# Causal masks added to the score banks by an identity matmul in a two-layer hybrid attention trunk

## Chip, cores and metric

The kernel runs on one core of one Trainium2 chip. The time is device microseconds of one execution of the whole program, the median of three runs. What the core has: TensorE (PE for its matmuls, PEld for the loads of their stationary operand), VectorE (DVE), ScalarE (ACT), GpSimd (POOL), SyncE (SP, which issues most DMAs here), SBUF, and eight PSUM banks of 128 partitions x 512 float32.

## The reference

A trunk of two layers on x of 512 rows x 1024 columns. In each layer: an RMSNorm and one input projection; from it four heads of differential attention with rotary (two softmax maps per head, subtracted) and eight heads of stick-breaking attention; the two results are projected, gated, merged and projected again; then a SwiGLU FFN. The two kinds of causal mask are what this change is about:

```python
# differential: a key may be the query itself
mask = kpos[None, :] <= qpos[:, None]
sc = einsum('bhqd,bhkd->bhqk', qb, k) * scale
w = softmax(where(mask, sc, -inf))
# stick-breaking: keys before the query only
mask = kpos[None, :] < qpos[:, None]
z = einsum('bhqd,bhkd->bhqk', qb, k) * scale
log_beta = log_sigmoid(z)
log_rem = where(mask, log_sigmoid(-z), 0.0)
after = cumsum(log_rem, reverse=True) - log_rem
a = where(mask, exp(log_beta + after), 0.0)
```

## The kernel before

All activations are kept transposed (features on partitions, the 512 tokens along the free axis). A projection is made in groups: 128 output features, eight steps of 128 input features, and for each step three float32r matmuls of 512 columns, because weight and activation are each split into a high and a low float32r part (L204: high x high, L205: weight low x high, L206: weight high x activation low). So a group is 24 matmuls. Its weight block comes by one DMA (L110), is rounded by ACT (L111) and its low part is made by DVE or, for some blocks, POOL (L113).

Attention goes by eight units a layer: four of the stick-breaking kind (s0 to s3, `class SB`), then four of the differential kind (d0 to d3, `class Diff`). A unit has two halves, c = 0 and 1. For each half, `scores` (L397) writes the causal part of the 512 x 512 score matrix, four blocks of rows of 128 queries with 128, 384, 512 and 256 keys, into three PSUM banks (L405 and L406: key high and key low; a query's two parts lie on the two halves of the partitions). Then `maps`:

- Stick-breaking (L428): ACT makes e = sigmoid(-z/8) and z = sigmoid(z/8) from the banks (L435, L437). POOL multiplies z on the four diagonal blocks with a 0/1 mask (L441). DVE runs a scan along e, from the last key to the first, with a second operand that holds it at 1 on masked places (L443). POOL multiplies z with the scanned e (L445).
- Differential (L472): DVE adds a mask of 0 and -1e30 to the diagonal blocks in PSUM (L481), takes row maxima (L482, L483), ACT exponentiates with row sums (L487), DVE and POOL scale (L489 to L496).

Two halves later (`LAG`), `mix` transposes the map on PE into three banks (L419), splits it (L422 on ACT, L423 on DVE), and multiplies it with the values (L456, L457; L512 to L514); the result is read by L461 (ACT) and L462 (DVE), or normalised through a matmul of ones (L525, L526) and L152 to L156. Projection groups of the next unit and of the gates stand between these steps as work for PE. Pools: five banks (`at`) for scores, transposes, values and norms together, three (`mm`) for projections, four buffers of the maps (`wk`).

The order of each engine's instructions is not the written one: a scheduler in the layer that records the kernel runs its own estimate of the timeline and lays each engine's queue down in that order. On the chip each engine goes through its queue in order. So taking instructions out, or putting some in, moves others.

Of the kernel before, what the change touches and what calls it, by code (L numbers as in the profile page):

```python
# [8 lines left out]
F32 = mybir.dt.float32  # L9
F32R = mybir.dt.float32r  # L10
BF16 = mybir.dt.bfloat16
AF = mybir.ActivationFunctionType
ALU = mybir.AluOpType
AX = mybir.AxisListType

P = 128
# [4 lines left out]
HID = 2816  # L21
NH = HID // P
EPS = 1e-6
NEG = -1.0e30


SEG = {0: (0, 0, 0, 128), 2: (0, 128, 128, 384), 3: (1, 0, 512, 512), 1: (2, 0, 1024, 256)}
# [20 lines left out]
def trunk(ctx: ExitStack, tc, xT, par, tab, scn, msk, w_in, w_o, w_out, w_fi, w_fo, out):  # L48
    nc = tc.nc
    cst = ctx.enter_context(tc.tile_pool(name="cst", bufs=1))  # L50
# [5 lines left out]
    def bank(tag, name):  # L56
        return psm.tile([P, 512], F32, name=name, tag=tag, bufs=BANK_BUFS[tag])
# [72 lines left out]
    ident = cst.tile([P, P], F32, name="ident")  # L130
# [95 lines left out]
            pass  # L226
    for k in range(KT):
        nrm.square(k)
    mk = cst.tile([P, 2, P], F32, name="mk")
    nc.sync.dma_start(out=mk, in_=msk)  # L230
    lam = cst.tile([P, DEPTH], F32, name="lam")
    gsub = cst.tile([P, DEPTH], F32, name="gsub")
    lctx = ExitStack()
    lcst = lctx.enter_context(tc.tile_pool(name="lcst", bufs=1))
    lpt = lcst.tile([P, DEPTH, 2, 2, 64], F32, name="lpt")
    nc.sync.dma_start(out=lpt.rearrange("p l a b d -> p (l a b d)"), in_=par[:, C_LP:])
    lpp = lcst.tile([P, DEPTH, 2, 64], F32, name="lpp")
    lps = lcst.tile([P, DEPTH, 2], F32, name="lps")
    for l in range(DEPTH):
# [6 lines left out]
                                       in1=lps[:, l, 0:1], op0=ALU.add, op1=ALU.subtract)  # L246
# [11 lines left out]
    def fbank(name):  # L258
        t = free_tags[fcount[0] % len(free_tags)]
        fcount[0] += 1  # L260
        return bank(t, name)

    for l in range(DEPTH):
        h = nrm.h
        with ExitStack() as ac:
# [10 lines left out]
            def T(tag, name, shape=(P, S), dt=F32):  # L276
                return ap_.tile(list(shape), dt, name=f"{name}_{l}", tag=tag, bufs=BUFS.get(tag, 1))
# [41 lines left out]
            class Unit:  # L319
# [77 lines left out]
                def scores(self, c):  # L397
                    ka, kl = self.k[c], self.k[2][c]
                    qs = self.q[c]
                    bs = [bank("at", f"s{self.n}{c}{i}_{l}") for i in range(3)]  # L400
                    for qb in (0, 2, 3, 1):
                        bi, c0, _, n = SEG[qb]
                        qc = slice(qb * P, qb * P + P)
                        dst = bs[bi][:, c0:c0 + n]
                        nc.tensor.matmul(dst, qs[:, qc], ka[:, 0:n], start=True, stop=False)  # L405
                        nc.tensor.matmul(dst, qs[:, qc], kl[:, 0:n], start=False, stop=True)  # L406
                    return bs

                def transposed(self, w, name):
# [17 lines left out]
            class SB(Unit):  # L427
                def maps(self, c):  # L428
                    name = f"{self.n}{c}"
                    bs = self.scores(c)  # L430

                    e = T("wk", "e" + name, (P, 1280))
                    z = T("wk", "z" + name, (P, 1280))
                    for i, (o, n) in enumerate(BANKS):
                        nc.scalar.activation(out=e[:, o:o + n], in_=bs[i][:, :n], func=AF.Sigmoid, scale=-0.125)  # L435
                    for i, (o, n) in enumerate(BANKS):
                        state["sig"] = nc.scalar.activation(out=z[:, o:o + n], in_=bs[i][:, :n], func=AF.Sigmoid,  # L437
                                                            scale=0.125)
                    for o in (0, 384, 896, 1152):
                        d = z[:, o:o + P]  # L440
                        nc.gpsimd.tensor_tensor(out=d, in0=d, in1=mk[:, 1], op=ALU.mult)  # L441

                    nc.vector.tensor_tensor_scan(out=e[:, ::-1], data0=e[:, ::-1], data1=msc[:, ::-1], initial=1.0,  # L443
                                                 op0=ALU.mult, op1=ALU.max)
                    nc.gpsimd.tensor_tensor(out=z[:, 0:1279], in0=z[:, 0:1279], in1=e[:, 1:1280], op=ALU.mult)  # L445
                    return z
# [24 lines left out]
            class Diff(Unit):  # L471
                def maps(self, c):  # L472
                    name = f"{self.n}{c}"
                    bs = self.scores(c)
                    p = T("wk", "p" + name, (P, 1280))
                    mx = T("mx", "mx" + name, (P, 4))
                    sm = T("sm", "sm" + name, (P, 4))
                    for qb in (0, 2, 3, 1):
                        bi, c0, s0, n = SEG[qb]
                        d = bs[bi][:, c0 + n - P:c0 + n]  # L480
                        nc.vector.tensor_tensor(out=d, in0=d, in1=mk[:, 0], op=ALU.add)  # L481
                        nc.vector.tensor_reduce(out=mx[:, qb:qb + 1], in_=bs[bi][:, c0:c0 + n], axis=AX.X, op=ALU.max)  # L482
                    nc.vector.tensor_scalar(out=mx, in0=mx, scalar1=-0.125, scalar2=None, op0=ALU.mult)  # L483
                    for qb in (0, 2, 3, 1):
                        bi, c0, s0, n = SEG[qb]
                        with tc.issue_after(state["tab"].ins):
                            nc.scalar.activation(out=p[:, s0:s0 + n], in_=bs[bi][:, c0:c0 + n], func=AF.Exp,  # L487
                                                 scale=0.125, bias=mx[:, qb:qb + 1], accum_out=sm[:, qb:qb + 1])
                    nc.vector.reciprocal(out=sm, in_=sm)  # L489
                    if c == 1:  # L490
                        nc.vector.tensor_scalar(out=sm, in0=sm, scalar1=lam[:, l:l + 1], scalar2=None, op0=ALU.mult)
                    else:
                        for qb in (0, 2, 3, 1):
                            bi, c0, s0, n = SEG[qb]
                            nc.gpsimd.tensor_scalar(out=p[:, s0:s0 + n], in0=p[:, s0:s0 + n],
                                                    scalar1=sm[:, qb:qb + 1], scalar2=None, op0=ALU.mult)  # L496
                    return p, sm
# [85 lines left out]
            for m in range(8):  # L583
                hi, lo = w_get(l, "o", m)
                bs, bd = fbank(f"ws{m}_{l}"), fbank(f"wd{m}_{l}")
# [88 lines left out]
def _constants(np):  # L674
    pos = np.arange(S, dtype=np.float32)
    inv = np.float32(10000.0) ** (-np.arange(0, 64, 2, dtype=np.float32) / np.float32(64))
    ang = pos[None, :] * inv.astype(np.float32)[:, None]
    cos, sin = np.cos(ang), np.sin(ang)
    tab = np.stack([np.concatenate([cos] * 4), np.concatenate([sin, -sin] * 2)], axis=1).astype(np.float32)
    q, k = np.arange(P)[:, None], np.arange(P)[None, :]  # L680
    msk = np.stack([np.where(k <= q, 0.0, NEG), np.where(k < q, 1.0, 0.0)], axis=1).astype(np.float32)
    scn = np.zeros((P, 1280), np.float32)
    for o in (0, 384, 896, 1152):
        scn[:, o:o + P] = 1.0 - msk[:, 1]
    return np.ascontiguousarray(tab), scn, np.ascontiguousarray(msk)


# [32 lines left out]
```

## Time and profile before

| | |
|---|---|
| median of 3 runs | 1538.57 us (1538.2 to 1538.72) |
| the profiled execution | 1538.29 us, of which its span, first to last instruction, 1536.5 us |
| PE busy in the span | 1482.3 us (96%), 6756 matmuls |
| DVE, ACT, POOL busy | 873.2 (57%), 611.3 (40%), 412.6 us (27%) |
| attention of layer 0, of layer 1 | about 45 to 300 us, about 790 to 1050 us |
| TensorE's clock over the span | 0.983 of full |

A time stands for a start in us from the first instruction, a duration beside it in us. A matmul's duration overlaps that of the next one, so what a matmul costs in a stream is the distance from its start to the next start. The clock has two levels, 2.4 GHz (1.0) and 1.2 GHz (0.5); a granted clock in between is a mean over a stretch.

### The profile page before, as it was taken

The numbers are of one execution on the slowest core, as the hardware profiler recorded it, in microseconds if no ns is written. First come the engines' busy times: TensorE is split into PE (matmuls) and PEld (weight loads), VectorE is DVE, ScalarE is ACT, GpSimd is POOL, SyncE is SP. The second block draws the span as 40 slices with busy tenths as digits, with TensorE's granted clock in tenths as the row PEclk, the third lists the DMA queues.
The fourth block names the chain that finished last, engine by engine and source line by source line (L and its number), as shares of the span: only waits on it lengthen the run. The fifth ranks groups of instructions, "written<-read, shape, count | busy, mean of one in ns | idle before, by whom it ended". The sixth has DMA issues, their size and how long they took to land.

```text
span 1536.5 us, 17374 instructions
## 1 busy us (share of the span) xinstructions
PE 1482.3 (96%) x6756; PEld 1228.0 (80%) x6756; DVE 873.2 (57%) x1070; ACT 611.3 (40%) x968; POOL 412.6 (27%) x288
## 2 busy tenths in 40 slices
PE   8899989999999999999997989999999999999997
PEld 6777778888888888888886867788888888888886
DVE  5978777565454544423367778765755454544223
ACT  5546445453332322322235645536434222333231
POOL 4679444000111111101128765520011111111011
PEclk8999999999999999999999999999999999999999
DMA  6212222223332323333331212322332323232331
GB/s 206 69 58 69 87 77 82 82 96 96 96 96 96 96 96 96 93 100 100 93 109 42 76 55 73 113 69 71 114 102 85 104 91 106 92 101 90 99 94 61
DMA packets 43619, 139.59 MB, mean 91 GB/s; under 512 B 5648, under 2 KB 8080, under 8 KB 43536
## 3 DMA queue, kind: packets, MB, share of 16 engines
q1 hardware_dynamic: 42240, 137.38, 28.7%
q8 instruction: 53, 0.87, 0.2%
q10 hardware_dynamic: 1296, 1.09, 0.2%
q14 instruction: 30, 0.25, 0.1%
HBM read 132.16 MB, written 2.10 MB: 87 GB/s over the span
## 4 chain that ended last, share of the span: by engine, by line
PE 79%; DVE 8%; POOL 5%; issue 3%; ACT 2%; DMA 1%; SPq 1%; DVEq 0%; POOLq 0%; ACTq 0%
PE fg L204 5%; PE fu L204 5%; PE fg L205 5%; PE fu L205 5%; PE fu L206 5%; PE fg L206 5%; PE fo L204 5%; PE fo L206 5%; PE fo L205 5%; PE pg L206 3%; PE pg L205 3%; PE pg L204 3%; PE wo L205 2%; PE wo L206 2%; PE wo L204 2%
## 5 line engine op out<-in xcount | busy, mean ns | idle before, releaser
L111 ACT CAST wh<-wr 128x1024 fp32r<-128x1024 f32 (+3 forms) x251 | 258.2, 1029 | 608.5 <-PE fu L206 153.6
L113 DVE TENSOR_TENSOR wl<-wr,wh 128x1024 fp32r<-128x1024 f32 (+2 forms) x229 | 327.7, 1431 | 208.1 <-ACT wh L111 207.6
L625 POOL TENSOR_TENSOR u<-u,g 128x512 f32<-128x512 f32 x44 | 57.9, 1316 | 440.4 <-DVE u L624 383.3
L205 PE MATMUL fo<-ah,wl 128*128 128x512 f32 (+1 forms) x374 | 141.0, 377 | 0.0
L204 PE MATMUL fo<-ah,wh 128*128 128x512 f32 (+1 forms) x374 | 141.0, 377 | 0.0
L206 PE MATMUL fo<-al,wh 128*128 128x512 f32 (+1 forms) x374 | 140.8, 376 | 0.0
L204 PE MATMUL fg<-hhf,wh 128*128 128x512 f32 x352 | 137.7, 391 | 0.0
L206 PE MATMUL fu<-hlf,wh 128*128 128x512 f32 x352 | 136.9, 389 | 0.0
L205 PE MATMUL fg<-hhf,wl 128*128 128x512 f32 x352 | 136.9, 389 | 0.0
L206 PE MATMUL fg<-hlf,wh 128*128 128x512 f32 x352 | 136.9, 389 | 0.0
L204 PE MATMUL fu<-hhf,wh 128*128 128x512 f32 x352 | 136.9, 389 | 0.0
L205 PE MATMUL fu<-hhf,wl 128*128 128x512 f32 x352 | 136.9, 389 | 0.0
L624 DVE TENSOR_TENSOR u<-fu,yf 128x512 f32<-128x512 f32 x44 | 30.4, 691 | 129.5 <-PE fu L206 129.5
L204 PE MATMUL pg<-hha,wh 128*128 128x512 f32 x256 | 101.4, 396 | 0.0
L206 PE MATMUL pg<-hla,wh 128*128 128x512 f32 x256 | 101.3, 396 | 0.0
L205 PE MATMUL pg<-hha,wl 128*128 128x512 f32 x256 | 101.3, 396 | 0.0
L205 PEld LDWEIGHTS fo<-ah,wl 128*128 128x128 f32 x374 | 70.4, 188 | 13.1
L206 PEld LDWEIGHTS fo<-al,wh 128*128 128x128 f32 x374 | 70.4, 188 | 13.0
L204 PEld LDWEIGHTS fo<-ah,wh 128*128 128x128 f32 x374 | 70.4, 188 | 12.7
L204 PE MATMUL pd<-hha,wh 128*128 128x512 f32 x192 | 77.1, 402 | 2.6 <-ACT knd3s L336 2.6
L113 POOL TENSOR_TENSOR wl<-wr,wh 128x1024 fp32r<-128x1024 f32 (+3 forms) x22 | 49.0, 2229 | 108.4 <-ACT wh L111 94.4
L187 POOL TENSOR_TENSOR accf<-accf,sqf 128x512 f32<-128x512 f32 x10 | 18.5, 1846 | 220.0 <-ACT sqf L185 220.0
(266 smaller groups left out, 3197.4 us busy)
## 6 DMA issues: line engine op xcount, KB each, us to landing
wr<-in_w_fi_dram SPq DMA_DIRECT2D x88, 512.0 KB, 3.5
wr<-in_w_in_dram SPq DMA_DIRECT2D x78, 512.0 KB, 3.5
wr<-in_w_fo_dram SPq DMA_DIRECT2D x32, 512.0 KB, 3.5
wr<-in_w_o_dram SPq DMA_DIRECT2D x16, 512.0 KB, 3.5
wr<-in_w_out_dram SPq DMA_DIRECT2D x16, 512.0 KB, 3.5
wr<-in_w_fo_dram SPq DMA_DIRECT2D x16, 384.0 KB, 3.1
x<-in_xT_dram SPq DMA_DIRECT2D x8, 256.0 KB, 5.3
cs<-in_tab_dram SPq DMA_DIRECT2D x2, 512.0 KB, 5.0
```

Of the source, the lines that this page charges most:

```text
L111: nc.scalar.copy(out=hi[:, c], in_=raw[:, c])
L113: eng.tensor_tensor(out=lo[:, c], in0=raw[:, c], in1=f32(hi[:, c]), op=ALU.subtract)
L187: eng.tensor_tensor(out=self.acc, in0=self.acc, in1=sq, op=ALU.add)
L204: nc.tensor.matmul(dst, hi[:, c], rh, start=first and k == 0, stop=False)
L205: nc.tensor.matmul(dst, lo[:, c], rh, start=False, stop=False)
L206: nc.tensor.matmul(dst, hi[:, c], rl, start=False, stop=last and k == n - 1)
L624: nc.vector.tensor_tensor(out=u, in0=bu, in1=r, op=ALU.mult)
L625: nc.gpsimd.tensor_tensor(out=u, in0=u, in1=g, op=ALU.mult)
```

## The change

The masks become one more matmul in each block of scores. `mk` is cast to float32r and holds 0 and -2^100 for both kinds (the stick-breaking one was 1 and 0); an identity in float32r, `identr`, is the stationary operand; behind the two score matmuls of each of the four row blocks a third one of 128 columns adds the mask to the diagonal block in PSUM. The POOL products (L441) and the DVE additions (L481) go. sigmoid and exp then give 0 or 1 on masked places by themselves. Two casts on ACT are added at the start.

```diff
--- before.py
+++ after.py
@@ -21,7 +21,7 @@
 HID = 2816
 NH = HID // P
 EPS = 1e-6
-NEG = -1.0e30
+NEG = -2.0 ** 100
 
 
 SEG = {0: (0, 0, 0, 128), 2: (0, 128, 128, 384), 3: (1, 0, 512, 512), 1: (2, 0, 1024, 256)}
@@ -226,12 +226,17 @@
             pass
     for k in range(KT):
         nrm.square(k)
-    mk = cst.tile([P, 2, P], F32, name="mk")
-    nc.sync.dma_start(out=mk, in_=msk)
     lam = cst.tile([P, DEPTH], F32, name="lam")
     gsub = cst.tile([P, DEPTH], F32, name="gsub")
     lctx = ExitStack()
     lcst = lctx.enter_context(tc.tile_pool(name="lcst", bufs=1))
+
+    mkf = lcst.tile([P, 2, P], F32, name="mkf")
+    nc.sync.dma_start(out=mkf, in_=msk)
+    mk = cst.tile([P, 2, P], F32R, name="mk")
+    nc.scalar.copy(out=mk, in_=mkf)
+    identr = cst.tile([P, P], F32R, name="identr")
+    nc.scalar.copy(out=identr, in_=ident)
     lpt = lcst.tile([P, DEPTH, 2, 2, 64], F32, name="lpt")
     nc.sync.dma_start(out=lpt.rearrange("p l a b d -> p (l a b d)"), in_=par[:, C_LP:])
     lpp = lcst.tile([P, DEPTH, 2, 64], F32, name="lpp")
@@ -403,7 +408,8 @@
                         qc = slice(qb * P, qb * P + P)
                         dst = bs[bi][:, c0:c0 + n]
                         nc.tensor.matmul(dst, qs[:, qc], ka[:, 0:n], start=True, stop=False)
-                        nc.tensor.matmul(dst, qs[:, qc], kl[:, 0:n], start=False, stop=True)
+                        nc.tensor.matmul(dst, qs[:, qc], kl[:, 0:n], start=False, stop=False)
+                        nc.tensor.matmul(dst[:, n - P:], identr, mk[:, int(self.kind == "s")], start=False, stop=True)
                     return bs
 
                 def transposed(self, w, name):
@@ -436,9 +442,6 @@
                     for i, (o, n) in enumerate(BANKS):
                         state["sig"] = nc.scalar.activation(out=z[:, o:o + n], in_=bs[i][:, :n], func=AF.Sigmoid,
                                                             scale=0.125)
-                    for o in (0, 384, 896, 1152):
-                        d = z[:, o:o + P]
-                        nc.gpsimd.tensor_tensor(out=d, in0=d, in1=mk[:, 1], op=ALU.mult)
 
                     nc.vector.tensor_tensor_scan(out=e[:, ::-1], data0=e[:, ::-1], data1=msc[:, ::-1], initial=1.0,
                                                  op0=ALU.mult, op1=ALU.max)
@@ -477,8 +480,6 @@
                     sm = T("sm", "sm" + name, (P, 4))
                     for qb in (0, 2, 3, 1):
                         bi, c0, s0, n = SEG[qb]
-                        d = bs[bi][:, c0 + n - P:c0 + n]
-                        nc.vector.tensor_tensor(out=d, in0=d, in1=mk[:, 0], op=ALU.add)
                         nc.vector.tensor_reduce(out=mx[:, qb:qb + 1], in_=bs[bi][:, c0:c0 + n], axis=AX.X, op=ALU.max)
                     nc.vector.tensor_scalar(out=mx, in0=mx, scalar1=-0.125, scalar2=None, op0=ALU.mult)
                     for qb in (0, 2, 3, 1):
@@ -678,10 +679,10 @@
     cos, sin = np.cos(ang), np.sin(ang)
     tab = np.stack([np.concatenate([cos] * 4), np.concatenate([sin, -sin] * 2)], axis=1).astype(np.float32)
     q, k = np.arange(P)[:, None], np.arange(P)[None, :]
-    msk = np.stack([np.where(k <= q, 0.0, NEG), np.where(k < q, 1.0, 0.0)], axis=1).astype(np.float32)
+    msk = np.stack([np.where(k <= q, 0.0, NEG), np.where(k < q, 0.0, NEG)], axis=1).astype(np.float32)
     scn = np.zeros((P, 1280), np.float32)
     for o in (0, 384, 896, 1152):
-        scn[:, o:o + P] = 1.0 - msk[:, 1]
+        scn[:, o:o + P] = msk[:, 1] != 0.0
     return np.ascontiguousarray(tab), scn, np.ascontiguousarray(msk)
```

Counts: 32 score halves (2 layers, 8 units, 2 halves) of four row blocks make 128 new matmuls with 128 new loads; 64 POOL and 64 DVE instructions go. (Lines behind L236 have other numbers in the changed kernel: L441 and L481 are gone, L445 is L448, L405 and L406 are L410 and L411, the mask is L412, L336 is L341, L487 is L488, L419 is L425, L526 is L527.)

What stands where, in three places. In a name such as zs01 the digits are the unit and the half, in ss102 the unit, the half and the bank; the number behind the last underscore is a buffer's.

POOL's queue in the first stick-breaking halves of layer 0, before:

```order
L376 TENSOR_TENSOR qbs0_0_343<-qns0_0_340,qbs0_0_343 64x512
L441 TENSOR_TENSOR zs00_0_372<-zs00_0_372,mk_192 128x128 x3
L375 TENSOR_TENSOR qas1_0_459<-qns1_0_457,qas1_0_459 64x512
L441 TENSOR_TENSOR zs00_0_372<-zs00_0_372,mk_192 128x128
L376 TENSOR_TENSOR qbs1_0_460<-qns1_0_457,qbs1_0_460 64x512
L441 TENSOR_TENSOR zs01_0_477<-zs01_0_477,mk_192 128x128 x2
L445 TENSOR_TENSOR zs00_0_372<-zs00_0_372,es00_0_371 128x1279
L441 TENSOR_TENSOR zs01_0_477<-zs01_0_477,mk_192 128x128 x2
L445 TENSOR_TENSOR zs01_0_477<-zs01_0_477,es01_0_476 128x1279
L375 TENSOR_TENSOR qas2_0_665<-qns2_0_663,qas2_0_665 64x512
L376 TENSOR_TENSOR qbs2_0_666<-qns2_0_663,qbs2_0_666 64x512
L441 TENSOR_TENSOR zs10_0_545<-zs10_0_545,mk_192 128x128 x4
```

and now:

```order
L381 TENSOR_TENSOR qbs0_0_347<-qns0_0_344,qbs0_0_347 64x512
L380 TENSOR_TENSOR qas1_0_463<-qns1_0_461,qas1_0_463 64x512
L381 TENSOR_TENSOR qbs1_0_464<-qns1_0_461,qbs1_0_464 64x512
L448 TENSOR_TENSOR zs00_0_380<-zs00_0_380,es00_0_379 128x1279
L448 TENSOR_TENSOR zs01_0_485<-zs01_0_485,es01_0_484 128x1279
L448 TENSOR_TENSOR zs10_0_553<-zs10_0_553,es10_0_552 128x1279
L380 TENSOR_TENSOR qas2_0_669<-qns2_0_667,qas2_0_669 64x512
L381 TENSOR_TENSOR qbs2_0_670<-qns2_0_667,qbs2_0_670 64x512
L113 TENSOR_TENSOR wl12_877<-wr12_875,wh12_876 128x1024
L448 TENSOR_TENSOR zs11_0_691<-zs11_0_691,es11_0_690 128x1279
```

The mask products are gone; the product with the scanned e stands directly behind the query splits (L380, L381).

ACT's queue at the differential unit d2 of layer 0, before (omd0 is the bank of d0's norm, pd30 a projection bank of d3, sd200 to sd202 the scores of d2's first half):

```order
L152 ACTIVATE yod0_0_1812<-omd0_0_1805,eps_81 128x512
L153 ACTIVATE yod0_0_1812<-yod0_0_1812 128x512
L336 COPY knd3s_0_1918<-pd30_0_1885 128x512
L487 ACTIVATE pd20_0_1864,smd20_0_1866<-sd200_0_1853,mxd20_0_1865 128x128
L487 ACTIVATE pd20_0_1864,smd20_0_1866<-sd200_0_1853,mxd20_0_1865 128x384
L487 ACTIVATE pd20_0_1864,smd20_0_1866<-sd201_0_1854,mxd20_0_1865 128x512
L487 ACTIVATE pd20_0_1864,smd20_0_1866<-sd202_0_1855,mxd20_0_1865 128x256
L336 COPY qnd3s_0_1968<-pd31_0_1935 128x512
L111 CAST wh29_2178<-wr29_2177 128x1024
```

and now:

```order
L152 ACTIVATE yod0_0_1816<-omd0_0_1809,eps_81 128x512
L153 ACTIVATE yod0_0_1816<-yod0_0_1816 128x512
L488 ACTIVATE pd20_0_1872,smd20_0_1874<-sd200_0_1857,mxd20_0_1873 128x128
L488 ACTIVATE pd20_0_1872,smd20_0_1874<-sd200_0_1857,mxd20_0_1873 128x384
L488 ACTIVATE pd20_0_1872,smd20_0_1874<-sd201_0_1858,mxd20_0_1873 128x512
L488 ACTIVATE pd20_0_1872,smd20_0_1874<-sd202_0_1859,mxd20_0_1873 128x256
L341 COPY knd3s_0_1922<-pd30_0_1889 128x512
L341 COPY qnd3s_0_1972<-pd31_0_1939 128x512
```

The exponentials of d2's first half moved ahead of the copy that frees the projection bank pd30.

PE's queue at the same place, from the second half's first scores to the projection group pd32, before:

```order
L405 MATMUL sd210_0_1983<-kbd2_0_1637,qbd2_0_1687 128x384
L406 MATMUL sd210_0_1983<-klz01_0_323,qbd2_0_1687 128x384
L526 MATMUL omd0_0_1805<-old0_0_1807,ones_v_79 128x512
L204 MATMUL pd32_0_2012<-hha00_110,wh25_1887 128x512
L205 MATMUL pd32_0_2012<-hha00_110,wl25_1888 128x512
L206 MATMUL pd32_0_2012<-hla00_111,wh25_1887 128x512
```

and now:

```order
L410 MATMUL sd210_0_1987<-kbd2_0_1641,qbd2_0_1691 128x384
L411 MATMUL sd210_0_1987<-klz01_0_327,qbd2_0_1691 128x384
L412 MATMUL sd210_0_1987<-mk_199,identr_201 128x128
L410 MATMUL sd211_0_1988<-kbd2_0_1641,qbd2_0_1691 128x512
L411 MATMUL sd211_0_1988<-klz01_0_327,qbd2_0_1691 128x512
L412 MATMUL sd211_0_1988<-mk_199,identr_201 128x128
L410 MATMUL sd212_0_1989<-kbd2_0_1641,qbd2_0_1691 128x256
L411 MATMUL sd212_0_1989<-klz01_0_327,qbd2_0_1691 128x256
L412 MATMUL sd212_0_1989<-mk_199,identr_201 128x128
L204 MATMUL pd32_0_2016<-hha00_110,wh25_1891 128x512
L205 MATMUL pd32_0_2016<-hha00_110,wl25_1892 128x512
```

The rest of the second half's scores (sd211, sd212), which stood 22 projection matmuls later, now stands ahead of pd32. Elsewhere: between the last score matmul of s1's first half and the first transposes of the kernel (of zs00), 12 projection matmuls stood before and 9 stand now.

## Rows read from the trace of the kernel before

**Rows 1.** Busy time by stretch, us: PE, PEld, DVE, ACT, POOL; clock; DMA; GB/s
```profile
45.00:150.00 105.00, 94.60 (x456) 78.41 (x455) 85.21 (x79) 60.82 (x114) 84.90 (x56) 0.93 0.19 61
150.00:300.00 150.00, 143.20 (x682) 119.11 (x681) 108.53 (x190) 67.40 (x144) 59.74 (x41) 0.97 0.27 81
790.00:910.00 120.00, 105.14 (x518) 86.66 (x518) 92.54 (x90) 64.90 (x120) 86.47 (x58) 0.97 0.22 70
910.00:1050.00 140.00, 132.49 (x636) 110.72 (x635) 102.50 (x184) 65.26 (x138) 58.01 (x39) 0.98 0.27 83
...
300.00:784.00 484.00, 484.00 (x2135) 400.39 (x2134) 225.54 (x242) 162.05 (x205) 52.44 (x37) 1.00 0.31 96
```
**Rows 2.** Waits of PE in the four attention stretches: us in total, times, longest
```profile
PE ts L419 <- POOL zs L445: 4.6, 1, 4.6
...
PE avs L457 <- DVE tls L423: 7.4, 3, 3.8
PE ts L419 <- POOL zs L445: 4.4, 1, 4.4
...
PE ts L419 <- DVE os L462: 2.7, 1, 2.7
PE sd L405 <- DVE os L462: 2.1, 1, 2.1
PE pd L204 <- ACT knd3s L336: 2.0, 1, 2.0
...
PE pd L204 <- ACT knd3s L336: 0.6, 1, 0.6
```
**Rows 3.** Timeline of PE behind the first stall: start, us, instruction
```profile
72.33 1.12 PE L419 MATMUL ts<-ident,zs 128*128 128x128 f32 x4 [4.64 <-POOL zs L445]
73.09 0.78 PE L206 MATMUL ps<-hla,wh 128*128 128x512 f32 x1
...
77.02 0.39 PE L206 MATMUL ps<-hla,wh 128*128 128x512 f32 x1
```
**Rows 4.** Timelines of DVE and POOL around two PE stalls
```profile
59.24 3.81 DVE L443 TENSOR_TENSOR_SCAN es<-es,msc 128x1280 f32<-128x1280 f32 x1 [1.70 <-ACT es L435]
...
60.45 2.86 POOL L441 TENSOR_TENSOR zs<-zs,mk 128x128 f32<-128x128 f32 x1
...
66.71 5.56 POOL L445 TENSOR_TENSOR zs<-zs,es 128x1279 f32<-128x1279 f32 x1
...
830.43 2.78 POOL L445 TENSOR_TENSOR zs<-zs,es 128x1279 f32<-128x1279 f32 x1
...
830.93 2.83 DVE L368 TENSOR_TENSOR klz<-kns,kbs 64x512 fp32r<-64x512 f32 x1
```
**Rows 5.** The mask products on POOL: times, duration in ns min/median/max
```profile
L441 POOL TENSOR_TENSOR zs<-zs,mk x64: 449/466/3303, 57.6 to 907.0; 128x128 f32<-128x128 f32 x64
```
**Rows 6.** Timeline of PE in the first scores of layer 0
```profile
52.74 0.22 PE L405 MATMUL ss<-kas,qas 128*128 128x128 f32 x1
52.80 0.28 PE L406 MATMUL ss<-klz,qas 128*128 128x128 f32 x1
52.91 0.39 PE L405 MATMUL ss<-kas,qas 128*128 128x384 f32 x1
```
**Rows 7.** Timelines of DVE and ACT in the first differential map
```profile
163.53 0.29 DVE L481 TENSOR_TENSOR sd<-sd,mk 128x128 f32<-128x128 f32 x1
163.72 0.68 DVE L482 TENSOR_REDUCE mxd<-sd 128x1 f32<-128x512 f32 x1
...
167.08 0.37 ACT L487 ACTIVATE pd<-sd,mxd 128x128 f32<-128x128 f32 x1 [7.90 <-DVE mxd L483]
...
169.10 0.62 ACT L373 CAST qad<-qnd 64x512 fp32r<-64x512 f32 x1
```
**Rows 8.** Timeline of ACT near the start: [idle before <- released by]
```profile
2.76 0.30 ACT L111 CAST wh<-wr 128x128 fp32r<-128x128 f32 x1 [0.32 <-DMA wr<-in_w_in_dram]
...
20.44 0.40 ACT L242 ACTIVATE lps<-lps 128x2 f32<-128x2 f32 x2 [3.99 <-DVE lps L241]
```

## The prediction

> **What bounds the kernel now.** I read the busy times by stretch first [rows 1]. Outside attention PE is busy without a gap at full clock (484.00 of 484 us between 300 and 784), so nothing there can be won, and the change touches nothing there. In the four attention stretches PE is idle for 105 - 94.60 = 10.4, 150 - 143.20 = 6.8, 120 - 105.14 = 14.9 and 140 - 132.49 = 7.5 us: 25.3 us in the stick-breaking parts (45 to 150 and 790 to 910), 14.3 us in the differential parts.
>
> The second thing to see in [rows 1] is the clock: 0.93, 0.97, 0.97 and 0.98. Behind the longest stalls PE goes on at the lower of its two levels. In [rows 3] nine matmuls of 512 columns take from 73.09 to 77.02, 3.93 us; at full clock 2135 matmuls take 484 us [rows 1], 0.227 us each, so nine take 2.04, and the stall of 4.64 us cost a further 1.9 us. Over the stretches the clock gives away 105 x 0.07 + 120 x 0.03 = 11.0 us in the stick-breaking parts and 150 x 0.03 + 140 x 0.02 = 7.3 in the differential ones. About 1 us of it falls on time in which PE was idle anyway, which leaves 10.4 and 6.9. So PE's stalls are worth 25.3 + 10.4 = 35.7 us in the stick-breaking parts and 21.2 us in the differential ones. That is all that a change to the masks' engines can win. What it costs is PE time, and PE is the bound.
>
> Third, who ends those waits [rows 2]: twice the product L445 on POOL (4.6 and 4.4), and for the rest mostly DVE: splits of transposes (7.4 in three waits between 790 and 910), the sums L462 (2.7 and 2.1 between 150 and 300). In the stick-breaking parts POOL is busy 84.9 of 105 and 86.5 of 120 us, DVE 85.2 and 92.5 [rows 1]: two loaded engines that stretch each other. The mask product takes 0.449 us at best and 3.303 at worst [rows 5]; a DVE instruction that starts inside a POOL product of 2.78 us is itself 2.83 us long [rows 4].
>
> **What the change adds on PE.** 128 matmuls of 128 columns in float32r, each with its own load. The nearest rows are the two 128-column score matmuls of the same type [rows 6]: the second starts 0.06 us behind the first, and the matmul behind it 0.11 us later. So a mask costs 0.06 us where the loads around it are hidden by long matmuls, 0.11 us where they aren't, as behind the 128-column block or where the next block's load is pushed back. Ends: 128 x 0.06 = 7.7 and 128 x 0.11 = 14.1 us. I take the middle, 0.085, 10.9 us, since 32 of them stand behind short blocks and the others push the next load. Below 7.7 it goes only if masks fall into stalls that last until another engine is ready; that is counted with the stalls.
>
> The Trainium skill, page "TensorE: Matmul & The Clock Gate", section "Back-to-back issue gap", gives about 81 ns for a matmul of 128 columns in a stream with its loads; by that the term would be an estimated 10.4 us, inside the ends above.
>
> **What it takes off POOL and DVE.** POOL loses 64 products, 64 x 0.466 = 30 us by the median, and more with what contention adds. In the first half of layer 0 the chain is plain: a mask product of 2.86 us at 60.45, the scan done at 59.24 + 3.81 = 63.05, L445 only at 66.71 and 5.56 us long [rows 4], the transposes at 72.33 [rows 3]. POOL's queue now has the query splits and then L445 directly. Without four masks on the way, L445 can start when the scan is done, 3.7 us earlier, and in an emptier stretch of DVE. So I take the two waits named POOL as gone, each with the 1.9 us of clock: 4.6 + 4.4 + 3.8 = 12.8 us.
>
> The rest of the stick-breaking stalls, 35.7 - 12.8 = 22.9 us, ends on DVE and ACT work that was late for a mixture of reasons: products in front of the query splits and of the rotary steps on POOL, DVE instructions stretched by POOL. The masks are one part of it. L445, which stays, is another: at 830.93 it was L445 and not a mask that stretched the DVE instruction ahead of the late split [rows 4]. I take half, 11.4 us. Ends: nothing and all of it. Together 24.2 us.
>
> **The differential parts.** The 64 DVE additions take 0.289 us each, but the next instruction starts 0.19 us later [rows 7], so a half wins 4 x 0.19 = 0.8 us on DVE's queue. Two PE waits hang on a DVE sum L462 in these stretches [rows 2]; in the first map it stands behind such additions: 1.6 us less.
>
> Against it stands d2. PE waits there for the copy that frees a projection bank (2.0 us in layer 0, 0.6 in layer 1) [rows 2]. Now four exponentials stand ahead of that copy on ACT; the first map's take from 167.08 to 169.10, 2.0 us [rows 7]. Of that PE spends about 0.9 us on the scores moved into the place. So the wait grows by 1.1 us a layer, 2.2 us, and layer 1's wait, then 1.7 us, may bring a lower clock for another 1.9. I take +3.1; the part as a whole +1.5 us, with ends -4 (the queue is ahead in more places) and +5.
>
> **The start.** Two casts are added on ACT. The identity's 128 x 128 cast costs 0.3 us by the row of the same shape and stands in an idle 0.32 us before the first weight cast; the mask's falls before a wait of 3.99 us [rows 8]. Both are hidden, at most 0.1 us late. The mask's DMA is the same one. FFN and projections behind attention keep their work: 0.
>
> **The sum.** The profiled execution is 1538.29 us (span 1536.5 and 1.8 around it), 0.3 below the median. +10.9 - 24.2 + 1.5 = -11.8, so 1526.5 us, beside the median 1526.8. I say 1527.
>
> **Rivals.** *The cover is taken back (slower).* The scheduler lays the queues by its own estimate, in which POOL's products may never have been late. It put the first transposes behind 9 projection matmuls instead of 12, some 0.7 us less cover, and crowded d2's scores. If new waits open in other places for all that closes, the stalls stay at 57 us, PE pays 10.9, the differential part 1.5: 1538.3 + 12.4 = 1551 us. It decides from the point where the stick-breaking stalls shrink by less than 12.4 us. For it speaks that stalls are set by an order made with wrong durations, against it that POOL had 81% load and now has half of that.
>
> *Only POOL's own two waits go.* The waits that end on DVE stay, since L445 still stretches DVE: 10.9 - 12.8 + 1.5 = -0.4, 1538 us. The Trainium skill, page "SBUF — State Buffer", section "Who interferes with whom", says that a VectorE instruction with two SBUF inputs and a GpSimd instruction that reads SBUF exclude each other for the whole instruction, whoever starts first; the 2.83 us at 830.93 agree, and by it the long POOL product goes on blocking as before.
>
> *Nearly all stick-breaking stalls go*, and the matmuls cost little: 9 - 34 - 2 = -27, 1511 us. For it speaks that POOL's queue feeds query splits, rotary steps and L445 alike.
>
> *It doesn't do what it says* is out: the order shows the 64 + 64 instructions gone and 128 matmuls there.
>
> **Chances.** About 0.2% (3 us) is what a measurement of this kernel can tell from no change. Forecast, 1518 to 1535: 0.42. Nearly all stalls gone, below 1518: 0.16. Only the two waits, 1535.5 to 1541.5: 0.14. Cover taken back, above 1541.5: 0.28. So faster 0.58, same 0.14, slower 0.28. Range: the low end is 10.9 - 35.7 less a few in the differential part, 1508; the high end the cover rival, 1551. About one in ten lies on either side.
>
> **What would show it.** In the changed kernel's waits of PE, the two named POOL zs should be gone, PE idle in the stick-breaking stretches should be about 11 instead of 25.3 us, with a clock of 0.97 or more; POOL's busy time should fall by 50 to 65 us. Mask matmuls should start 0.06 to 0.11 us before the next matmul. At d2 PE should wait 2 to 3 us for the copy or the exponentials. It is wrong if PE's idle time in attention stays near 40 us, or if a mask costs over 0.11 us.

## The result and the profile after

The changed kernel takes 1526.28 us (median; 1523.85 to 1527.29), the kernel before 1538.38 in the same comparison: 0.9921 of the time, 95% interval 0.9904 to 0.9938. Forecast were 1527. The profiled execution has a span of 1525.0 us (before 1536.5), TensorE's mean clock is 0.988 (0.983). The total came out as forecast; the terms did not, and most of what follows is about that.

The page's first part for the changed kernel, busy us by engine:

```profile
PE 1488.5 (98%) x6884; PEld 1238.6 (81%) x6884; DVE 853.7 (56%) x1006; ACT 614.4 (40%) x970; POOL 347.4 (23%) x224
```

POOL lost 65.2 us, DVE 19.5. The stretches of [rows 1] again, in the same columns:

```profile
45.00:150.00 105.00, 98.32 (x505) 83.55 (x504) 85.35 (x85) 61.56 (x115) 53.94 (x26) 0.95 0.20 61
150.00:300.00 150.00, 147.94 (x731) 124.62 (x731) 99.83 (x161) 75.55 (x153) 57.37 (x38) 0.99 0.27 85
790.00:910.00 120.00, 110.72 (x560) 92.65 (x558) 95.72 (x96) 67.30 (x128) 62.04 (x33) 0.96 0.21 65
910.00:1050.00 140.00, 137.93 (x678) 116.37 (x677) 92.47 (x144) 69.73 (x139) 50.87 (x32) 0.99 0.27 82
```

PE's idle time is now 6.7 and 9.3 us in the stick-breaking stretches (25.3 together before, 16.0 now) and 2.1 and 2.1 in the differential ones (14.3 before, 4.1 now). The larger part of the idle time that went was in the parts where the prediction expected none to go. Who ends PE's waits (us in total, times, longest; compare [rows 2]):

```profile
PE avs L460 <- DVE tls L429: 7.9, 4, 3.0
PE ts L425 <- DVE vs L398: 4.0, 1, 4.0
PE sd L410 <- ACT pd L488: 3.6, 2, 1.8
...
PE ss L410 <- DVE vs L398: 1.6, 1, 1.6
...
PE ts L425 <- POOL zs L448: 0.5, 1, 0.5
PE pd L204 <- ACT knd3s L341: 0.5, 2, 0.2
```

The two waits named POOL zs (4.6 and 4.4) have shrunk to one of 0.5. The large ones left end on DVE. Two DVE timelines of the changed kernel (start, us; the second is in layer 1), and the POOL products beside them:

```profile
64.56 2.56 DVE L371 CAST kbs<-kns 64x512 fp32r<-64x512 f32 x1
...
69.72 2.83 DVE L446 TENSOR_TENSOR_SCAN es<-es,msc 128x1280 f32<-128x1280 f32 x1
72.46 0.40 DVE L398 TENSOR_TENSOR vs<-vts,vs 128x256 fp32r<-128x256 f32 x1
...
73.65 4.17 DVE L446 TENSOR_TENSOR_SCAN es<-es,msc 128x1280 f32<-128x1280 f32 x1
...
813.67 2.26 DVE L370 CAST kas<-kns 64x512 fp32r<-64x512 f32 x1
815.94 0.42 DVE L371 CAST kbs<-kns 64x512 fp32r<-64x512 f32 x1
...
819.30 2.83 DVE L446 TENSOR_TENSOR_SCAN es<-es,msc 128x1280 f32<-128x1280 f32 x1
822.04 0.67 DVE L429 TENSOR_TENSOR tls<-ts,ths 128x512 fp32r<-128x512 f32 x1
```

```profile
64.32 2.52 POOL L448 TENSOR_TENSOR zs<-zs,es 128x1279 f32<-128x1279 f32 x1
...
813.20 2.45 POOL L448 TENSOR_TENSOR zs<-zs,es 128x1279 f32<-128x1279 f32 x1 [3.96 <-DVE es L446]
```

The small instruction that PE waits for, a value split (L398) or a transpose split (L429), stands behind a scan of 2.8 us. In layer 0 a second value split hangs on the first through a cast on ACT (72.89, which had waited 4.94 us for it), and the transposes follow at 73.87. POOL is idle meanwhile (5.85 us up to 72.69, 6.64 up to 822.29), so the order in DVE's queue has a part in these waits. But POOL has one too, some microseconds earlier: the key splits at 64.56 and 813.67 start inside a product L448 and take 2.56 and 2.26 us, where a key split of the same size at 815.94, with POOL idle, takes 0.42. DVE has no pause from there to the split that PE waits for, so up to 2.1 and 1.8 us of the two waits can be POOL's. No run takes the two shares apart.

### The profile page after: what moved, and what is told of

The parts are those of the page before. It is cut to its first block, busy times and chain, and to the rows that moved or that the text cites. A ratio compares the mean times of both kernels' runs of the same rounds, so it can differ in the third digit from the quotient of the medians.

```text
span 1525.0 us, 17531 instructions
## 1 busy us (share of the span) xinstructions
PE 1488.5 (98%) x6884; PEld 1238.6 (81%) x6884; DVE 853.7 (56%) x1006; ACT 614.4 (40%) x970; POOL 347.4 (23%) x224
## 4 chain that ended last, share of the span: by engine, by line
PE 90%; DVE 5%; issue 1%; ACT 1%; DMA 1%; POOL 0%; SPq 0%; DVEq 0%; POOLq 0%; ACTq 0%
PE fu L206 5%; PE fg L205 5%; PE fg L206 5%; PE fu L205 5%; PE fg L204 5%; PE fu L204 5%; PE fo L204 5%; PE fo L205 5%; PE fo L206 5%; PE pg L204 4%; PE pg L205 4%; PE pg L206 4%; PE pd L204 3%; PE pd L205 3%; PE pd L206 3%; PE wo L204 2%
## 5 line engine op out<-in xcount | busy, mean ns | idle before, releaser
L205 PE MATMUL pd<-hha,wl 128*128 128x512 f32 x192 | 77.7, 405 | 0.0
```

The lines of the kernel that those rows point to most:

```text
L205: nc.tensor.matmul(dst, lo[:, c], rh, start=False, stop=False)
```

## The experiments

Four theories were set against each other: the products taken off POOL (A); the additions taken off DVE (B); the order in which the scheduler lays the queues down, which any edit moves (C); that the work alone decides, whatever the order (W). The before that each time is set against was run beside it (1537.1 to 1538.0 us). Executions of one kernel lie 1 to 7 us apart, so a few microseconds between two of the kernels below are little.

**One half of the change.** Masks by matmul in the stick-breaking units alone, the DVE additions kept:

```diff
-nc.tensor.matmul(dst, qs[:, qc], kl[:, 0:n], start=False, stop=False)
-nc.tensor.matmul(dst[:, n - P:], identr, mk[:, int(self.kind == "s")], start=False, stop=True)
+nc.tensor.matmul(dst, qs[:, qc], kl[:, 0:n], start=False, stop=self.kind != "s")
+if self.kind == "s":
+    nc.tensor.matmul(dst[:, n - P:], identr, mk[:, int(self.kind == "s")], start=False, stop=True)
...
```

> Only the stick-breaking masks go by the matmul (64 of 128); the differential ones stay additions on DVE. Theory A (the prediction's: the gain is POOL's relief in the stick-breaking parts): 5.4 us of PE for -24, about 1520 us. Theory B (from the two traces: idle time of PE fell by 9 us in the stick-breaking parts, by 10 us and most of the lower clock in the differential ones, so the DVE additions were what counted): -9 + 5.4, about 1534 us. Theory C (the new order of the queues counts, not the work taken off): any value, and the changes of this run and of e2_diff_only don't add up to that of the whole change (-12 us).

Measured: 1516.8 us, 0.9859 (0.9842 to 0.9875), 9.5 us better than the whole change. And the reverse, with `"d"` for `"s"` and the POOL products kept:

> Only the differential masks go by the matmul; the stick-breaking ones stay products on POOL. Theory A: PE pays 5.4 us and 1.5 come on top, about 1545 us. Theory B: -15 + 5.4, about 1529 us. Theory C: no sum with e1_stick_only.

Measured: 1536.4 us, 0.9993 (0.9983 to 1.0002), no change. PE's waits for the POOL product are both there (first line layer 0, second layer 1):

```profile
PE ts L428 <- POOL zs L454: 5.0, 1, 5.0
...
PE ts L428 <- POOL zs L454: 4.4, 1, 4.4
```

The halves give -20.8 and -1.2, together -22, the whole change -12: they do not add up. Of the forecasts, A's for the first half (1520) was met, A's for the second (1545) and both of B's (1534 and 1529) were not. PE's waits of the first half alone in layer 0 (45 to 300 us):

```profile
PE ts L426 <- DVE vs L398: 4.0, 1, 4.0
PE pd L204 <- ACT knd3s L341: 2.0, 1, 2.0
PE avs L461 <- DVE tls L430: 1.9, 2, 1.7
PE ts L426 <- POOL zs L449: 0.3, 1, 0.3
```

Nothing there ends on the sums any more (L462 in [rows 2]), although all DVE additions are still in place: B falls for the differential stalls.

**The change with the old work put back.** First all 64 POOL products (they multiply by 1 or 0 what is masked already), then all 64 DVE additions:

```diff
...
+for o in (0, 384, 896, 1152):
+    d = z[:, o:o + P]
+    nc.gpsimd.tensor_tensor(out=d, in0=d, in1=m01, op=ALU.mult)
```

> The changed kernel with the 64 POOL products on the diagonal blocks put back as well (they multiply what is already 0). So PE pays for all masks and POOL has no relief. Theory A: the gain of 24 us is gone, about 1551 us. Theory B: only the differential gain stays, about 1534 us.

Measured: 1530.39 us, 0.9953 (0.9937 to 0.9968).

```diff
+d = bs[bi][:, c0 + n - P:c0 + n]
+nc.vector.tensor_tensor(out=d, in0=d, in1=f32(mk[:, 0]), op=ALU.add)
```

> The changed kernel with the 64 DVE additions put back as well (the mask is added twice). Theory A: +2 us, about 1528 us. Theory B: the differential gain of 15 us is gone, about 1541 us.

Measured: 1522.28 us, 0.9904 (0.9889 to 0.9919). A had forecast 1551 and 1528, B 1534 and 1541. The first is the differential half (1536.4) with 64 more matmuls in it, and 6 us faster than that; the second is the changed kernel with 64 more additions, and 4 us faster than that, 3 us if each is set against its own before, with intervals that overlap. The work added can't explain a gain; the queues of both stand in another order. But little of it is idle time of PE (the table below has 2.7 us less in the first, 1.0 us more in the second); the rest is a better clock, in the second 0.98, 0.97, 1.00 and 1.00 in the four windows of the table (two stick-breaking, two differential), against 0.95, 0.95, 0.99 and 0.99 in the changed kernel. So the second shows neither work nor order. In it, PE's wait at d2 is 0.5 us in each layer, for the copy, against 1.8 for the exponentials in the changed kernel. Against the stick-breaking half it has 64 masks more, and is 5.5 us slower; that is no clean price of a mask either, since the half ran at a lower clock (0.95, 0.95, 0.99 and 1.00).

**The order alone.** Two edits that change no instruction, only the sequence in which they are written, and with it the scheduler's order (616 and 602 rows of PE's queue differ in the kernel before):

```diff
-                    for qb in (0, 2, 3, 1):
+                    for qb in (0, 2, 1, 3):
```

> The kernel before with the same instructions; only the written order of the last two row blocks in the scores is swapped (0, 2, 1, 3), which makes the scheduler lay the queues down otherwise (616 rows of PE's queue differ). Theory W (the work taken off or added counts): within 3 us of 1537.5. Theory C (the order of the queues counts as much): more than 4 us away, to either side.

> The changed kernel with the swap of o1_before_scores_order. Theory W: within 3 us of 1526 and 11 us below o1_before_scores_order. Theory C: the distance to o1_before_scores_order is not 11 us but anything between 0 and 25.

```diff
-                    for i, kbs in enumerate(((0,), (1, 3), (2,))):
+                    for i, kbs in ((0, (0,)), (2, (2,)), (1, (1, 3))):
```

> The kernel before with the same instructions; only the three banks of the transposes are written in the order 0, 2, 1 (602 rows of PE's queue differ). Theory W: within 3 us of 1537.5. Theory C: more than 4 us away.

> The changed kernel with the swap of o2_before_transposes_order. Theory W: within 3 us of 1526 and 11 us below o2_before_transposes_order. Theory C: the distance to o2_before_transposes_order is not 11 us but anything between 0 and 25.

> The kernel with masks by matmul in the stick-breaking part alone (1516.8 with the order as written), with the row blocks of a head's scores written in the order 0, 2, 1, 3 instead of 0, 2, 3, 1. The work is the same to the last instruction; the order of the queues is another. If the gain of 21 us over the kernel before comes from the work taken off GpSimd, it stays: 1513 to 1521. If it is to a good part a lucky order, as the runs of the two kernels with this swap suggest (the kernel before 1542, the changed one 1534), then the time moves toward theirs: 1523 to 1533.

> The same kernel with the three banks of the transposes written in the order 0, 2, 1. This swap took the kernel before from 1538 to 1523 and left the changed kernel at 1526. If what the swap gives and what the smaller change gives were separate, they would add up: 1517 - 15 = 1502. If both remove the same stalls, or the order alone decides, the time lies at 1513 to 1526. Slower than 1530 would say that this part of the change has no gain of its own over the kernel before with the same swap (1523).

Measured, with all other kernels. PE's idle us are the length less PE's busy time of the windows that begin with the first score matmul of the first stick-breaking or differential unit of a layer, and end with that of the next kind or the output projection, both layers together, in the profiled execution of each kernel:

| kernel | us | ratio to before (95%) | idle, stick-breaking | idle, differential |
|---|---|---|---|---|
| before | 1538.4 | | 25.2 | 14.4 |
| before, scores order | 1542.4 | 1.0023 (1.0013 to 1.0033) | 23.5 | 19.4 |
| before, transposes order | 1523.2 | 0.9903 (0.9889 to 0.9918) | 21.1 | 10.6 |
| changed | 1526.3 | 0.9921 (0.9904 to 0.9938) | 16.0 | 4.1 |
| changed, scores order | 1533.6 | 0.9979 (0.9968 to 0.9989) | 17.0 | 11.8 |
| changed, transposes order | 1526.0 | 0.9918 (0.9903 to 0.9933) | 15.9 | 6.7 |
| stick-breaking half | 1516.8 | 0.9859 (0.9842 to 0.9875) | 15.6 | 3.4 |
| same, scores order | 1535.4 | 0.9990 (0.9980 to 0.9999) | 16.9 | 19.5 |
| same, transposes order | 1516.5 | 0.9868 (0.9854 to 0.9883) | 15.2 | 7.3 |
| differential half | 1536.4 | 0.9993 (0.9983 to 1.0002) | 21.3 | 9.4 |
| products kept | 1530.4 | 0.9953 (0.9937 to 0.9968) | 19.0 | 9.0 |
| additions kept | 1522.3 | 0.9904 (0.9889 to 0.9919) | 16.6 | 4.5 |

Three things are to be read from it. The order alone moves the kernel before by 19 us (1523.2 to 1542.4), more than the change does; W falls and C stands. Over the three orders the change is worth -12.1, -8.8 and +2.8 us, its stick-breaking half -20.8, -7.0 and -6.6 (each to the kernel before with the same order; from different comparisons, in which before itself differs by up to 1.3 us). The +2.8 is no difference clear of noise, since the two intervals overlap; the half's -7.0 and -6.6 are, and are about -5 each by the ratios. And one column doesn't care for the order: PE's idle time in the stick-breaking parts is 19.0 to 25.2 us in the five kernels with the POOL products and 15.2 to 17.0 in the seven without (17.8 in the kernel with no masks, below). That much of A is shown: the products cost PE 5 to 10 us of idle time there in each of the three orders, and 3 us where they were put back into the changed kernel. The waits by name say the same. Those of the transposes for POOL's zs sum to 5.3 to 9.4 us in the five kernels with the products, and to 0.9 at most in the seven without. In their place the transposes of all seven wait 4.0 to 5.6 us in layer 0 for the value split (L398); of the five, two have such a wait, of 2.8 and 8.1 us. The differential column goes from 3.4 to 19.5 with the order, and is worst under the scores order in all three families. What the change does to it can't be told apart from the order.

The transposes order took 15 us off the kernel before and left both POOL waits in it (layer 0, layer 1):

```profile
PE ts L419 <- POOL zs L445: 5.0, 1, 5.0
...
PE ts L419 <- POOL zs L445: 4.4, 1, 4.4
```

**What a mask costs on PE.** In the feed-forward groups, where PE never waits, two additions of a 128-column tile of zeros to each of 88 groups:

```diff
...
             nc.tensor.matmul(dst, hi[:, c], rl, start=False, stop=last and k == n - 1 and not extra)
+            if extra and k in (3, 7):
+                nc.tensor.matmul(dst[:, 384:], identr, zer, start=False, stop=last and k == n - 1)
```

> The changed kernel, with two further matmuls in each of the 88 fg and fu groups of the feed-forward part: the identity times a tile of zeros of 128 columns, added into the last 128 columns of the bank, once among the group's matmuls and once at its end. They are 176 additions of the mask's size and form, in a stretch in which PE waits for nothing, and the order on every engine is otherwise that of the changed kernel. So their whole price must show in the time. The prediction's value of 0.085 us each gives 176 x 0.085 = +15.0 us over the changed kernel's 1526, its lower end of 0.06 gives +10.6, its upper end of 0.11 gives +19.4. That the whole change's PE cost of about 12.5 us was worked out rightly from the attention segments (0.098 a mask) wants +17; if additions of this size were nearly free (below 0.04, under +7), then the cost of the change sits elsewhere in attention and the saving of the stalls was smaller than taken.

Measured: 1545.54 us, 1.0059 (1.0044 to 1.0074): +19.3 us on the changed kernel's median (21 by the two ratios), 0.11 to 0.12 each, at the upper end of the forecast or just above it. The trace says more. PE's timeline in it (start, us):

```profile
420.65 0.39 PE L206 MATMUL fu<-hlf,wh 128*128 128x512 f32 x1
420.88 0.22 PE L208 MATMUL fu<-zer,identr 128*128 128x128 f32 x1
420.93 0.45 PE L204 MATMUL fu<-hhf,wh 128*128 128x512 f32 x1
421.22 0.39 PE L205 MATMUL fu<-hhf,wl 128*128 128x512 f32 x1
421.45 0.40 PE L206 MATMUL fu<-hlf,wh 128*128 128x512 f32 x1
```

The matmul behind the addition starts 0.05 us later, but the one behind that 0.29 later instead of 0.23: 0.11 us of the price show in these two steps, most of it one step on. (A load takes 0.19 us, and an addition that short may cover little of the next one; no run tests that.) From the first fg to the last fu matmul of a layer PE takes 240.01 us in the changed kernel (401.05 to 641.06) and 252.44 here (400.10 to 652.54), in both layers the same: 12.43 / 88 = 0.141 us an addition, 24.9 in all. The 0.03 us beyond the two steps is spread over the matmuls that follow, which start 0.229 us apart (421.22 to 423.51, ten steps) and not 0.227. The time rose by less, mostly because layer 1's attention gave 4.4 us back, with the queues in the same order and no less idle time (the changed kernel's window, then this one's):

```profile
791.80:897.30 105.50, 96.22 (x480) 80.15 (x479) 85.35 (x78) 58.72 (x110) 52.41 (x25) 0.95 0.20 64
```

```profile
803.20:904.30 101.10, 91.83 (x481) 76.31 (x480) 83.68 (x78) 57.75 (x108) 50.76 (x25) 1.00 0.21 68
```

PE is idle 9.28 and 9.27 us; the clock is 0.95 in one and 1.00 in the other.

**No masks at all:**

```diff
-                        nc.tensor.matmul(dst[:, n - P:], identr, mk[:, int(self.kind == "s")], start=False, stop=True)
```

> The changed kernel without the 128 mask matmuls, so that no causal mask is applied in either kind of layer; all else is as in the changed kernel. It takes off the whole PE cost of the masks, but the order of the queues moves with it. If 128 x 0.085 to 0.11 us were all: 1512 to 1515 from 1526. If the order decides as much as the work, anywhere from 1503 to 1527; the stalls that are left in it are those that masks have no part in, and PE's waits for GpSimd's products can't be among them.

Measured: 1511.98 us, 0.9835 (0.9821 to 0.985), 14.3 below the changed kernel, with more idle time (17.8 and 7.1 us) and a better clock (0.96, 0.98, 1.00, 1.00 in its four windows). The stick-breaking half alone, with half of the masks in it, is 5 us behind that.

## Why the prediction was right, and where it was wrong

**What a mask costs** (forecast 0.085 us, 10.9 in all; ends 7.7 and 14.1): inside the ends, but near the upper one. The four row blocks of a half, in the changed kernel, and the first score matmuls of the next half:

```profile
52.30 0.22 PE L410 MATMUL ss<-kas,qas 128*128 128x128 f32 x1
...
52.97 0.22 PE L412 MATMUL ss<-mk,identr 128*128 128x128 f32 x1
53.03 0.44 PE L410 MATMUL ss<-kas,qas 128*128 128x512 f32 x1
53.31 0.39 PE L411 MATMUL ss<-klz,qas 128*128 128x512 f32 x1
...
53.95 0.27 PE L410 MATMUL ss<-kbs,qbs 128*128 128x128 f32 x1
54.06 0.28 PE L411 MATMUL ss<-klz,qbs 128*128 128x128 f32 x1
```

and in the kernel before, which starts these blocks at 52.74 [rows 6]:

```profile
54.02 0.22 PE L405 MATMUL ss<-kbs,qbs 128*128 128x128 f32 x1
54.08 0.27 PE L406 MATMUL ss<-klz,qbs 128*128 128x128 f32 x1
```

As a mask's price falls one matmul later, the length to take is that to the second matmul of the next half: 54.06 - 52.30 = 1.76 us, before 54.08 - 52.74 = 1.34. So 0.42 us a half, 0.105 a mask, and 32 x 0.42 = 13.4 us if all halves are like this one, 2.5 us above the forecast. Behind a mask that projection matmuls follow, the two next starts (185.08, 185.14, 185.42 in the changed kernel) give 0.06 + 0.28 - 0.23 = 0.11 us. The sign that the prediction named for it (a mask starts 0.06 to 0.11 us before the next matmul) was met and is no proof, since the price falls one matmul later. The page of the Trainium skill that the prediction cites ("TensorE: Matmul & The Clock Gate", "Back-to-back issue gap") gives 81 ns for a matmul of 128 columns in a stream with its loads. Measured are 105 ns here among scores, and 141 in a stream of 512 columns, which is above the 0.11 us at which the prediction called itself wrong; what a mask costs where it stands is at that or just below.

**The stick-breaking stalls** (forecast -24.2): too much. (The clock's part in it was summed a little high: 94.60 x 0.07 + 105.14 x 0.03 is 9.8 us and not 10.4, which takes 0.3 off the 24.2.) Idle time fell by 9.2 us, from 25.2 to 16.0, not to 11; the clock, forecast at 0.97 or more, is 0.95 in both windows, and gives away 10.1 us against 10.3. So about -9.4. The two POOL waits went, as forecast; L445, now L448, which was up to 5.56 us long [rows 4], takes 2.45 to 2.52 each time:

```profile
L448 POOL TENSOR_TENSOR zs<-zs,es x16: 2447/2449/2515, 64.3 to 891.4; 128x1279 f32<-128x1279 f32 x16
```

Two steps failed. The POOL waits were taken as gone with nothing late behind them; but in place of the 4.64 us at 72.33 [rows 3] there are now 4.0 at 73.87, for the value split. And half of the rest, which ends on DVE, was taken to go with POOL's load; but POOL kept two thirds of it (53.9 + 62.0 of 84.9 + 86.5 us, not half), and the longest of these waits in layer 1, 3.8 us for the transpose split [rows 2], is still 3.0. L448 stretches a key split ahead of it, as L445 did at 830.93 [rows 4], and a scan of 2.83 us stands between.

**The differential parts** (forecast +1.5): wrong by 17 us. At d2 PE waits 1.8 us for the exponentials and 0.2 for the copy, in both layers: 2.0 us, as the prediction's sign wanted, though that is no growth in layer 0 and 1.4 us in layer 1, where 1.1 each were forecast. The step that failed is the rest, put at -1.6 us: idle time fell by 10.3 us, and with it 5 us of clock (0.97 and 0.98 to 0.99 and 0.99). Two pieces of it are the waits for the sums L462 in layer 0 (2.7 and 2.1 [rows 2]); the prediction gave them 1.6 us for the additions, but they are gone in the stick-breaking half too, with all additions in place. The largest piece is a wait in layer 1 of the kernel before. PE's line, POOL's timeline ahead of it, then DVE's:

```profile
925.25 0.80 PE L456 MATMUL avs<-ths,vs 128*128 128x512 f32 x1 [5.49 <-ACT pd L487]
```

```profile
906.97 0.46 POOL L441 TENSOR_TENSOR zs<-zs,mk 128x128 f32<-128x128 f32 x1
907.51 2.45 POOL L445 TENSOR_TENSOR zs<-zs,es 128x1279 f32<-128x1279 f32 x1
909.91 1.75 POOL L337 TENSOR_TENSOR knd1u<-knd1s,cs 128x512 f32<-128x512 f32 x1
918.05 1.29 POOL L342 TENSOR_TENSOR knd<-knd,knd1s 128x512 f32<-128x512 f32 x1 [6.38 <-DMA knd1s<-knd1u]
```

```profile
919.38 1.48 DVE L365 CAST kad<-knd 64x512 fp32r<-64x512 f32 x1 [2.53 <-POOL knd L342]
...
923.98 0.16 DVE L483 TENSOR_SCALAR mxd<-mxd 128x4 f32<-128x4 f32 x1
```

The last stick-breaking products hold up d1's rotary step on POOL (L337), POOL then waits 6.4 us for the transfer behind that step, and d1's key splits, which wait for what follows, stand on DVE and ACT ahead of the maxima and exponentials of d0. In the changed kernel the same steps on POOL:

```profile
891.42 2.46 POOL L448 TENSOR_TENSOR zs<-zs,es 128x1279 f32<-128x1279 f32 x1 [4.58 <-DVE es L446]
895.01 1.29 POOL L342 TENSOR_TENSOR knd1u<-knd1s,cs 128x512 f32<-128x512 f32 x1 [1.14 <-ACT knd1s L341]
900.90 1.28 POOL L347 TENSOR_TENSOR knd<-knd,knd1s 128x512 f32<-128x512 f32 x1 [4.59 <-DMA knd1s<-knd1u]
```

Now POOL waits for the copy, not the copy for POOL: against the first differential scores of the layer (906.5 before, 897.3 now) the rotary step starts 2.3 us ahead instead of 3.4 behind. The stick-breaking half alone has the same picture (the step at 891.99, its scores at 894.3). The prediction named this queue ("query splits, rotary steps and L445 alike") and booked it all to the stick-breaking parts. That the stall vanished in the kernel before with the transposes order too, with all products in place, says that the order could do it as well; how much of the 15 us is one and how much the other stays open.

**The sum.** Over the four windows, 546.1 us before and 534.6 now: -9.4 in the stick-breaking parts, -15.3 in the differential ones, +13.4 for the masks, -11.3 worked out and -11.5 measured (the clock's two digits are worth 2.7 us). Forecast were -24.2 + 1.5 + 10.9 = -11.8. Two errors of 15 to 17 us cancelled. The forecast was right on the sign of the stick-breaking term and near on the price, wrong on the sign of the differential term, and lucky on the total.

**The rivals.** "Only POOL's two waits go" had a mechanism that is still there, and the size wrong. It rests on a VectorE instruction with two SBUF inputs and a GpSimd instruction that reads SBUF shutting each other out (the Trainium skill, "SBUF — State Buffer", "Who interferes with whom"). The trace agrees: a scan that takes 2.83 us alone takes 4.17 when it starts, at 73.65, inside L448 (72.69 to 75.14). With a third of POOL's load gone fewer instructions meet it, but a key split stretched beside L448 stands ahead of both waits shown above. "The cover is taken back" came partly true: the new wait of 4.0 us is of its kind. What none of the cases had is that the order moves the time by 19 us with no work changed, an effect that the range from 1508 to 1551 was not worked out from.

## What to carry to other kernels

Where a scheduler lays the queues by its own estimate, one pair of times says little about an edit: write the same work in two or three other orders and compare families. Here that turned a gain of 12 us into a change of -12 to +3, and showed that the stick-breaking half of the change is the better kernel in two orders of three, by 9.5 us each, and 1.8 us worse in the third, within the noise. Moving small work onto the bound engine pays where it frees a queue that feeds it, POOL here; on the differential side, where 64 additions lay on an engine with room, it cost some 6.7 us of PE time (64 x 0.105), and no order shows a gain in time clear of noise for it.

The best kernel of the study that keeps all masks is the stick-breaking half with masks by matmul and the additions kept: 1516.8 us, or 1516.5 with the transposes order.

## What was not expected of the hardware

A 128-column matmul between 512-column ones costs 0.141 us, though the next starts 0.05 us behind it: the start-to-start distance of the instruction itself shows 0.05 of it, the next one another 0.06, and only the length of the whole stream all of it. And the clock does not follow idle time closely: the same queues with 9.28 and 9.27 us of idle time ran at 0.95 and 1.00 in layer 1's stick-breaking part, a difference of 4.4 us between two kernels that are alike there. A stall's price in clock (1.9 us a stall in the prediction) is no constant to be added up; why the two differ stays open.
